# One core, a Mamba-2 and stick-breaking block with SwiGLU: all first products of two gate/up quads run behind the last out_proj block, whose norm and tail go first, and the last tails get buffers of their own

## The chip, the cores and the metric

The kernel runs on one core of a Trainium2 chip. The metric is the device time of one execution in microseconds (us); the kernel before takes 1240.92 us, the median of three runs. In the profile the engines are PE (TensorE, matmuls), PEld (its weight loads), DVE (VectorE), ACT (ScalarE), POOL (GpSimd) and SP (SyncE, which here issues loads). L12 is line 12 of the kernel's file.

## What is computed

The reference is one layer on x of 1024 x 1024 in float32. What lies around the change is its second half:

```python
mix = jnp.concatenate([y_ssd, y_sb], axis=-1) @ w_out[layer]
x = x + rms_norm(mix, post_mix_gain[layer])

h = rms_norm(x, pre_ffn_gain[layer])
f = (jax.nn.silu(h @ w_gate[layer]) * (h @ w_up[layer])) @ w_down[layer]
x = x + rms_norm(f, post_ffn_gain[layer])
```

`y_ssd` is the output of a Mamba-2 scan, `y_sb` that of stick-breaking attention; both are done when the part that matters here begins. w_out is 1024 x 1024, w_gate and w_up are 1024 x 2816, w_down is 2816 x 1024.

## The kernel before, in words

**Numbers and products.** Every operand of a large product is split in two: a cast to a shorter float on ACT gives the high part `hi` (L72), a subtraction on DVE gives the rest `lo` (L73). A product of two such operands is three matmuls, hi·hi, hi·lo and lo·hi, into the same PSUM bank (`mm3`, L76 to L78). So each split costs one ACT and one DVE instruction, and PE cannot start before both.

**Order.** The program is written for a scheduler that places each engine's instructions by their dependencies and by a priority, which is by default the order in which the code is written. Every engine then works through its own list in order and waits by semaphores. Two things alter the order: `tc.high_priority(offset=n)` gives the instructions under it the priority of code written n instructions earlier, and `tc.issue_after(i)` keeps them behind instruction i. SP's list consists of the loads, POOL's of the stores, among other work. A load waits in SP's list until its buffer is free and, where it reads back what was stored, until that store has landed; the loads behind it wait with it.

**out_proj, norms and tails.** The output projection runs in eight blocks of 128 rows, p = 0 to 7, from the last rows of the sequence to the first. `run(p, ...)` is 48 matmuls into two banks `po`, with weights `woh`/`wol` and inputs `yhl`. `out_norm(p)` is a generator in three parts, with a `yield` between them:

1. squares of the product on ACT with row sums (L1035);
2. the inverse root of the row mean (`row_rstd`, the small steps `e`, `y`, `v`, `t`, `r` on ACT and DVE, L859 to L864), then per half the scaling by it and by the gain (DVE, L1041), the addition to x (DVE, L1042) and the squares for the second norm (ACT, L1043), and the store of the new x (POOL, L1044);
3. a second `row_rstd`, and the scaling by the second norm (DVE, L1049), which gives the tile `tm`, kept as `ts[p]`.

`out_tail(sb, ...)` turns block sb = p round: eight PE transposes into two banks `pt` (L1063), copied by ACT into `hT` (L1064). Tails 0 to 3 fill the columns of the operands B11 and B21 and store `hT` to `h2_d` in memory. Tails 4 to 7 load those blocks back as `b11` and `b21` (SP, L1076), form sums and differences with them on DVE (L1078, L1079, L1082, L1083), split two results into T2 and T3, and store three more to `late_d` on POOL (L1077, L1084, L1085). `b11` and `b21` have one buffer each, in the pool `op`, which all four tails share in turn. Tail p - 2 is written behind `run(p)`.

**Gate and up.** h @ w_gate and h @ w_up are made in quads of 256 columns by a scheme of seven products in place of eight (Strassen's). A quad runs once for gate (`g`) and once for up (`u`), and `step(p)` carries both one stage on. One stage is 12 matmuls for each of the two: `pa` = weights times B11, then a second product with B21 into the same bank; `pb` with T2; `pc` with T3; `pe` with T1; then T4 into the bank of `pc`, and B22 into that of `pe`. DVE adds up the parts as they come: `u2` (L911), `u3` (L917 and L921), and the two others (L925, L929). Four results of each quad leave through `gate`: Silu on ACT (L1004), a multiplication on DVE (L1005) and a store on POOL (L1006).

The left operands come from `lops`, a list of split weight blocks. The first four are those of quad 0's first two products, made by `early_ops` from the buffers `er` (loads at L1020, splits into `eo`). All others are made by `left_gen`, which `pump(n)` carries on until n pairs are ready: quad 1's first four from `head` (loads at L940), the rest from `fraw` (loads at L954), with DVE sums `fs` (L966, L967, L970, L972). T1, T4 and B22 are loaded back from `late_d` at the end of this part and split there (L1142 and the line behind it).

**PSUM.** `bank` hands out the eight banks in a fixed ring, two tagged mm, two z, one o and three px; `ring_i` counts them. A bank whose last reader is not through holds up the next product on it.

**The order written out.** Before the change, quad 0's first product `step(0)` stands ahead of block 7, the last; then `run(7)`, tail 5, part 1 of norm 7, the second product of quad 0 (`a00`), `pump(1)`, part 2 of norm 7, tail 6, part 3, `pump(2)`, quad 1's first product `step(1)`, tail 7, the gates. Tail 7 feeds T2, and with it the product `pb` of both quads.

Of the kernel before, what the change touches and what calls it, by code (L numbers as in the profile page):

```python
# [8 lines left out]
F32 = mybir.dt.float32  # L9
# [3 lines left out]
ALU = mybir.AluOpType  # L13
# [3 lines left out]
P = 128  # L17
# [3 lines left out]
NB = S // P  # L21
# [18 lines left out]
SIDE = 1  # L40
WARM = 12
LOOK = 4
# [5 lines left out]
def tile_hybrid_block(  # L48
# [19 lines left out]
    f32 = lambda ap: ap.bitcast(F32)  # L68

# [5 lines left out]
    def mm3(ps, ah, al, bh, bl, start, stop, more=False):  # L75
        T.matmul(ps, lhsT=ah, rhs=bh, start=start, stop=False, skip_group_check=more)  # L76
        T.matmul(ps, lhsT=ah, rhs=bl, start=False, stop=False, skip_group_check=more)  # L77
        T.matmul(ps, lhsT=al, rhs=bh, start=False, stop=stop, skip_group_check=more)  # L78
# [819 lines left out]
    def quad(p, name):  # L898
# [12 lines left out]
        V.tensor_tensor(p1, b, p1, ALU.add)  # L911
# [5 lines left out]
        V.tensor_tensor(u3, c, u2, ALU.add)  # L917
# [61 lines left out]
    def pump(n):  # L979
        while len(lops) < 2 * n:  # L980
            try:
                next(lg)
            except StopIteration:
                break
# [26 lines left out]
    with es_o:  # L1011
# [39 lines left out]

        def out_tail(sb, t):
# [21 lines left out]
            b11, b21 = [op.tile([P, 4, P], F32, tag=x, name=x, bufs=1) for x in ("b11", "b21")]  # L1074
# [23 lines left out]
        for p in range(NB):  # L1098
            if p == NB - 1:
                step(0)  # L1100
            run(p, "late" if p < 2 else "all")
            if p > 1:
                out_tail(p - 2, ts.pop(p - 2))
            norm = out_norm(p)
            if p < NB - 1:
                for _ in norm:
                    pass
            if 2 < p + 2 < NB:
                out_load(p + 2, "all")
            if p == 5:  # L1110
                early_ops()
        es_w.close()
        fw = ctx.enter_context(tc.tile_pool(reuse_waits="tile", name="fw", bufs=1, side="right"))
# [3 lines left out]
        next(norm)  # L1117
        a00 = step(0)
        pump(1)
        next(norm)  # L1120
        out_tail(6, ts[6])
        pump(2)
        next(norm, None)

        ring_i[0] += 4
        step(1)
        out_tail(7, ts[7])
# [9 lines left out]
    for i, op in enumerate((T1, T4, B22)):  # L1137
        if i == 1:
            pump(3)
        for c in range(4):  # L1140
            hi, lo = [x[:, :, P * c : P * c + P] for x in op]
            nc.sync.dma_start(f32(lo), late_d[i][c])  # L1142
            split(hi, lo, f32(lo))

# [229 lines left out]
```

## Time and profile before

| what | value |
|---|---|
| three runs | 1241.06, 1240.9, 1240.92 us (median 1240.92) |
| the profiled execution, its own time | 1240.09 us |
| its span | 1238.4 us |
| mean granted clock of TensorE | 0.989 |

The span is that of the engines' records and leaves out 1.7 us of the execution around them. The stretch that the change moves runs from about 568 to 650 us of the span. Rows of the trace are given as start, busy time (both in us), engine, line, operation, what it writes and what it reads, shape; xN joins N instructions on one row, and a bracket at the end gives the idle time of the engine ahead of it and what ended it. A row that joins several instructions has the sum of their times.

### The profile page before, as it was taken

Reading aid. Unit: us, or ns where it says so; the run is one execution under the profiler, and the core shown is the slowest. Engines: PE = TensorE matmul, PEld = TensorE weight load, DVE = VectorE, ACT = ScalarE, POOL = GpSimd, SP = SyncE. Lnnn points to the kernel's source line nnn. Section 1 sums busy time; section 2 is a strip of 40 time slices with the busy share of each in tenths; the row PEclk is TensorE's granted clock in tenths of the full one; section 3 lists DMA queues with packets and bytes.
Section 4 is the critical chain, followed back from the end, with each engine's and each line's share of the span. In section 5 each row is a group of like instructions: output and inputs, shape, how many; then the busy total and the mean of one; then the engine's idle time right before and its main releaser. Section 6 shows DMA issues by size and latency. Waiting matters only on the chain.

```text
span 1238.4 us, 16320 instructions
## 1 busy us (share of the span) xinstructions
PE 1192.9 (96%) x5641; PEld 972.5 (79%) x5641; DVE 931.1 (75%) x1461; ACT 587.2 (47%) x1115; POOL 92.2 (7%) x232
## 2 busy tenths in 40 slices
PE   9998999999999998999799999999999999999997
PEld 7776778787887775787678888888888888888885
DVE  7478988778997888667898555566655558998777
ACT  7247555555654667445553333333233335444543
POOL 0041110010110100011200000000000000000000
PEclk9999999999999999999999999999999999999998
DMA  6693252445557425855773223222233198133247
GB/s 193 193 353 112 71 153 74 139 118 178 151 167 197 136 83 185 232 179 176 263 220 104 76 79 102 77 85 80 65 102 97 67 325 319 62 126 104 101 136 237
DMA packets 139882, 183.23 MB, mean 148 GB/s; under 512 B 10660, under 2 KB 94852, under 8 KB 139800
## 3 DMA queue, kind: packets, MB, share of 16 engines
q1 hardware_dynamic: 128544, 151.18, 39.8%
q0 software_dynamic: 7424, 25.17, 5.6%
q10 hardware_dynamic: 3832, 5.84, 1.3%
q8 instruction: 44, 0.72, 0.2%
q14 instruction: 38, 0.31, 0.1%
HBM read 132.23 MB, written 49.92 MB: 147 GB/s over the span
## 4 chain that ended last, share of the span: by engine, by line
PE 70%; DVE 11%; issue 8%; DMA 5%; ACT 4%; SPq 1%; POOL 1%; DVEq 0%; ACTq 0%; POOLq 0%
PE pd L76 5%; PE pd L78 5%; PE pd L77 5%; DVE sn L569 3%; PE o L592 2%; PE tp L580 2%; PE pj_x L76 2%; PE pj_x L78 2%; PE pcg L76 2%; PE pj_x L77 2%; PE pcg L77 2%; PE pcg L78 2%; PE pcu L77 2%; PE peu L77 2%; PE peg L77 2%
## 5 line engine op out<-in xcount | busy, mean ns | idle before, releaser
L72 ACT CAST flhi<-fraw 128x512 fp32r<-128x512 f32 x102 | 62.7, 621 | 168.2 <-PE pcg L77 39.6
L76 PE MATMUL pd<-fohi 128*128 128x512 f32 x260 | 101.3, 389 | 0.0
L77 PE MATMUL pd<-folo,fohi 128*128 128x512 f32 x260 | 101.2, 389 | 0.0
L78 PE MATMUL pd<-fohi,folo 128*128 128x512 f32 x260 | 101.2, 389 | 0.0
L569 DVE TENSOR_TENSOR_SCAN sn<-sn,smask 128x1024 f32<-128x1024 f32 (+3 forms) x64 | 87.3, 1365 | 17.6 <-ACT sn L565 17.4
L73 DVE TENSOR_TENSOR fllo<-fraw,flhi 128x512 fp32r<-128x512 f32 x102 | 69.5, 685 | 34.9 <-ACT flhi L72 34.9
L565 ACT ACTIVATE sn<-zp,msc 128x512 f32<-128x512 f32 (+2 forms) x96 | 55.9, 585 | 34.6 <-PE zp L564 28.9
L72 ACT CAST fohi<-rt 128x512 fp32r<-128x512 f32 x83 | 48.8, 618 | 47.9 <-PE pd L77 28.0
L584 ACT CAST wh<-tp 128x512 fp32r<-128x512 f32 (+1 forms) x80 | 42.6, 544 | 38.6 <-PE tp L580 38.1
L73 DVE TENSOR_TENSOR folo<-rt,fohi 128x512 fp32r<-128x512 f32 x83 | 54.8, 682 | 6.5 <-ACT fohi L72 6.5
L72 ACT CAST flhi<-fs 128x512 fp32r<-128x512 f32 x44 | 27.2, 622 | 67.5 <-PE peg L77 33.5
L585 DVE TENSOR_TENSOR wl<-tp,wh 128x512 fp32r<-128x512 f32 (+1 forms) x80 | 49.6, 628 | 10.8 <-ACT wh L584 10.2
L566 ACT ACTIVATE sp<-zp,msc 128x512 f32<-128x512 f32 (+2 forms) x96 | 55.8, 583 | 2.5 <-PE tp L580 2.4
L78 PEld LDWEIGHTS pd<-fohi,folo 128*128 128x128 f32 x260 | 48.8, 188 | 10.2
L77 PEld LDWEIGHTS pd<-folo,fohi 128*128 128x128 f32 x260 | 48.8, 188 | 10.1
L76 PEld LDWEIGHTS pd<-fohi 128*128 128x128 f32 x260 | 48.8, 188 | 10.1
L580 PE MATMUL tp<-ident,sp 128*128 128x128 f32 x288 | 48.0, 278 | 5.7 <-DVE sp L570 5.1
L76 PE MATMUL po<-woh,yhl 128*128 128x512 f32 x128 | 50.9, 398 | 1.8 <-ACT yhl L72 1.3
L1006 POOL DMA_DIRECT2D a_d<-sg x44 | 23.7, 540 | 382.6 <-DVE sg L1005 382.6
L76 PE MATMUL pj_x<-hh,wh_x 128*128 128x512 f32 x128 | 52.2, 408 | 0.0
L78 PE MATMUL po<-woh,yhl 128*128 128x512 f32 x128 | 50.7, 397 | 0.5 <-DVE yhl L73 0.5
L78 PE MATMUL pj_x<-hh,wl_x 128*128 128x512 f32 x128 | 51.1, 399 | 0.0
(425 smaller groups left out, 3469.1 us busy)
## 6 DMA issues: line engine op xcount, KB each, us to landing
ps<-a_d SPq DMA_DIRECT2D x55, 256.0 KB
fraw<-in_w_gate_dram SPq DMA_DIRECT2D x22, 512.0 KB
fraw<-in_w_up_dram SPq DMA_DIRECT2D x22, 512.0 KB
a_d<-sg POOLq DMA_DIRECT2D x44, 256.0 KB, 2.6
rt<-in_w_down_dram SPq DMA_DIRECT2D x33, 256.0 KB
rt<-a_d SPq DMA_DIRECT2D x22, 256.0 KB
ps<-in_w_down_dram SPq DMA_DIRECT2D x22, 256.0 KB
xt<-in_x_t_dram SPq DMA_DIRECT2D x8, 512.0 KB
```

The costliest lines, as they stand in the source:

```text
L72: A.copy(hi, src)
L73: V.tensor_tensor(lo, src, f32(hi), ALU.subtract)
L76: T.matmul(ps, lhsT=ah, rhs=bh, start=start, stop=False, skip_group_check=more)
L77: T.matmul(ps, lhsT=ah, rhs=bl, start=False, stop=False, skip_group_check=more)
L78: T.matmul(ps, lhsT=al, rhs=bh, start=False, stop=stop, skip_group_check=more)
L565: A.activation(sn[:, 1 + off : 1 + off + cw_], zp[:, 0:cw_], AF.Sigmoid, scale=rqn[:, qb : qb + 1])
L566: A.activation(sp[:, off : off + cw_], zp[:, 0:cw_], AF.Sigmoid, scale=rqp[:, qb : qb + 1])
L569: V.tensor_tensor_scan(sn[:, 1 : 1 + W], sn[:, 1 : 1 + W], smask[:, 0:W], 1.0, ALU.mult, ALU.max)
L580: T.transpose(tp[:, P * i : P * i + P], ws[a][:, co : co + P], ident)
L584: A.copy(wh[:, 0:n_], tp[:, 0:n_])
L585: V.tensor_tensor(wl[:, 0:n_], tp[:, 0:n_], f32(wh[:, 0:n_]), ALU.subtract)
L592: T.matmul(o[:, 0:cw_], lhsT=vv[:, k, h, :], rhs=wt[:, c0 : c0 + cw_], start=(first and k == kb + 1 and wt is wh), stop=(last and k == kb ...
```

## The change

- Block 7's matmuls move ahead of quad 0's first product, and tail 5 with them: now `run(7)`, part 1 of norm 7, tail 5, `step(0)`, part 2, tail 6, part 3, then `step(0)`, `pump(2)`, `step(1)`, tail 7 and the gates.
- The three parts of norm 7 have a raised priority (150), and so has tail 7, which is kept behind the last matmul written so far.
- Tails 5, 6 and 7 take `b11` and `b21` from a new pool `op2` with two buffers each.
- The twelve loads of T1, T4 and B22 are issued together. The splits of T4 and of B22 are put further back: each behind `pump(1 + LOOK)`, a step of quad 0 with its gate, and the last DVE addition of that step.
- The ring of banks skips two places instead of four.

```diff
+URGENT = 150
...
-        T.matmul(ps, lhsT=al, rhs=bh, start=False, stop=stop, skip_group_check=more)
+        last_mm[0] = T.matmul(ps, lhsT=al, rhs=bh, start=False, stop=stop, skip_group_check=more)
...
         product(b, lops[x], T2, True)
-        V.tensor_tensor(p1, b, p1, ALU.add)
+        evac[0] = V.tensor_tensor(p1, b, p1, ALU.add)
...
-        V.tensor_tensor(u3, c, u2, ALU.add)
+        evac[0] = V.tensor_tensor(u3, c, u2, ALU.add)
...
-            b11, b21 = [op.tile([P, 4, P], F32, tag=x, name=x, bufs=1) for x in ("b11", "b21")]
+            late = op2[0] if op2 else op
+            b11, b21 = [late.tile([P, 4, P], F32, tag=x, name=x, bufs=2 if op2 else 1) for x in ("b11", "b21")]
...
-        for p in range(NB):
-            if p == NB - 1:
-                step(0)
+        for p in range(NB - 1):
             run(p, "late" if p < 2 else "all")
             if p > 1:
                 out_tail(p - 2, ts.pop(p - 2))
-            norm = out_norm(p)
-            if p < NB - 1:
-                for _ in norm:
-                    pass
+            for _ in out_norm(p):
+                pass
             if 2 < p + 2 < NB:
                 out_load(p + 2, "all")
             if p == 5:
                 early_ops()
+
+        run(NB - 1, "all")
         es_w.close()
+        op2.append(es_o.enter_context(tc.tile_pool(reuse_waits="tile", name="op2", bufs=2, side="left")))
...
-        next(norm)
+        norm = out_norm(NB - 1)
+        with tc.high_priority(offset=URGENT):
+            next(norm)
+        out_tail(5, ts.pop(5))
+        step(0)
+        with tc.high_priority(offset=URGENT):
+            next(norm)
+        out_tail(6, ts[6])
+        with tc.high_priority(offset=URGENT):
+            next(norm, None)
         a00 = step(0)
-        pump(1)
-        next(norm)
-        out_tail(6, ts[6])
         pump(2)
-        next(norm, None)
-
-        ring_i[0] += 4
         step(1)
-        out_tail(7, ts[7])
+        with tc.high_priority(offset=URGENT), tc.issue_after(last_mm[0].ins):
+            out_tail(7, ts[7])
+
+        ring_i[0] += 2
...
     for i, op in enumerate((T1, T4, B22)):
-        if i == 1:
-            pump(3)
+        for c in range(4):
+            nc.sync.dma_start(f32(op[1][:, :, P * c : P * c + P]), late_d[i][c])
+
+    def late_split(op):
         for c in range(4):
             hi, lo = [x[:, :, P * c : P * c + P] for x in op]
-            nc.sync.dma_start(f32(lo), late_d[i][c])
             split(hi, lo, f32(lo))
...
+    late_split(T1)
+    for op in (T4, B22):
+        pump(1 + LOOK)
+        gate(step(0))
+        with tc.issue_after(evac[0].ins):
+            late_split(op)
```

The changed file has two to seven more lines ahead of these places, so that L1041 becomes L1043 there, L1049 becomes L1051, L1063 becomes L1067, L1076 becomes L1081, L1079 becomes L1084, L1083 becomes L1088, L76 becomes L78 and L1142 becomes L1149.

PE, behind block 6's matmuls. `pt_5874` and `pt_5880` are tail 4's two banks, `pag` the bank of quad 0's first gate product, `po_59..` block 7's. Before, quad 0 comes first:

```order
L1063 MATMUL pt_5874<-ident_66,tm_5635 128x128 x4
L1063 MATMUL pt_5880<-ident_66,tm_5635 128x128 x4
L76 MATMUL pag_5937<-B11h_5118,eo_5801 128x512
L77 MATMUL pag_5937<-B11l_5119,eo_5801 128x512
L78 MATMUL pag_5937<-B11h_5118,eo_5802 128x512
```

After the change block 7 follows tail 4:

```order
L1067 MATMUL pt_5874<-ident_66,tm_5635 128x128 x4
L1067 MATMUL pt_5880<-ident_66,tm_5635 128x128 x4
L78 MATMUL po_5937<-woh0_4966,yhl_5786 128x512
L79 MATMUL po_5937<-wol0_4967,yhl_5786 128x512
L80 MATMUL po_5937<-woh0_4966,yhl_5786 128x512
```

The 24 matmuls of quad 0's first product have moved from ahead of block 7's 48 to behind them and behind tail 5's transposes.

DVE, in norm 7, from its additions to x (L1042, after L1044) to the scaling by the second norm (L1049, after L1051). `pt_6118`, `hT_6116` and `b21_6131` are tail 6's, `fs` are sums of quad 0's weights, `sg_6224` the multiplication of a gate. Before:

```order
L1042 TENSOR_TENSOR x1_6052<-x1_6052,tm_6055 128x512 x2
L1079 TENSOR_TENSOR pt_6118<-pt_6124,b11_6130 128x512
L1082 TENSOR_TENSOR hT_6116<-hT_6116,b11_6130 128x512
L861 SCALAR_TENSOR_TENSOR v_6153<-ssq2_6108,e_6156 128x1
L966 TENSOR_TENSOR fs_6274<-fraw_6266,fraw_6268 128x512
L73 TENSOR_TENSOR T2l_5123<-pt_6118,T2h_5122 128x4x128
L73 TENSOR_TENSOR T3l_5125<-pt_6124,T3h_5124 128x4x128
L1083 TENSOR_TENSOR b21_6131<-b21_6131,pt_6118 128x512
L862 SCALAR_TENSOR_TENSOR t_6155<-y0_6154,v_6153 128x1
L967 TENSOR_TENSOR fs_6275<-fs_6274,fraw_6266 128x512
L864 SCALAR_TENSOR_TENSOR r_6161<-t_6155,y0_6154 128x1
L1005 TENSOR_TENSOR sg_6224<-pau_5952,sg_6224 128x512
```

After the change; `pt_6004`, `pt_6010` and `b21_6017` are tail 5's, `pt_6087` is tail 6's, `head_6144` quad 1's first weight block:

```order
L1044 TENSOR_TENSOR x1_5997<-x1_5997,tm_6000 128x512 x2
L75 TENSOR_TENSOR T2l_5123<-pt_6004,T2h_5122 128x4x128
L75 TENSOR_TENSOR T3l_5125<-pt_6010,T3h_5124 128x4x128
L863 SCALAR_TENSOR_TENSOR v_6108<-ssq2_6071,e_6111 128x1
L1088 TENSOR_TENSOR b21_6017<-b21_6017,pt_6004 128x512
L864 SCALAR_TENSOR_TENSOR t_6110<-y0_6109,v_6108 128x1
L1083 TENSOR_TENSOR pt_6087<-pt_6087,hT_6079 128x512
L866 SCALAR_TENSOR_TENSOR r_6116<-t_6110,y0_6109 128x1
L75 TENSOR_TENSOR fllo_6153<-head_6144,flhi_6152 128x512
L1051 SCALAR_TENSOR_TENSOR tm_6000<-x1_5997,r_6116,g2_b_5132 128x512 x2
```

Eight large instructions stood inside norm 7 between these two points, five do now; most of tail 6 and the gate's multiplication have moved behind it, tail 5's end has moved in.

SP, from the last load of `er` on. Before:

```order
L1076 DMA b11_6030<-h2_d0_1_140 128x512
L1076 DMA b21_6031<-h2_d1_1_144 128x512
L940 DMA head_6082<-in_w_gate_dram 128x4x128
L940 DMA head_6083<-in_w_up_dram 128x4x128
L940 DMA head_6084<-in_w_gate_dram 128x4x128
L940 DMA head_6085<-in_w_up_dram 128x4x128
L954 DMA fraw_6266<-in_w_gate_dram 128x4x256
L1076 DMA b11_6130<-h2_d0_2_141 128x512
L954 DMA fraw_6268<-in_w_gate_dram 128x4x256
L954 DMA fraw_6270<-in_w_up_dram 128x4x256
L954 DMA fraw_6272<-in_w_up_dram 128x4x256
L1076 DMA b21_6131<-h2_d1_2_145 128x512
```

After:

```order
L1081 DMA b11_6016<-h2_d0_1_140 128x512
L1081 DMA b21_6017<-h2_d1_1_144 128x512
L1081 DMA b11_6093<-h2_d0_2_141 128x512
L1081 DMA b21_6094<-h2_d1_2_145 128x512
L942 DMA head_6144<-in_w_gate_dram 128x4x128
L942 DMA head_6145<-in_w_up_dram 128x4x128
L942 DMA head_6146<-in_w_gate_dram 128x4x128
L1081 DMA b11_6212<-h2_d0_3_142 128x512
L942 DMA head_6147<-in_w_up_dram 128x4x128
L956 DMA fraw_6270<-in_w_gate_dram 128x4x256
L956 DMA fraw_6272<-in_w_gate_dram 128x4x256
L956 DMA fraw_6274<-in_w_up_dram 128x4x256
```

Tail 6's loads now stand right behind tail 5's, ahead of the weights of both quads, and tail 7's `b11` among quad 1's; before, each of them waited for the buffer of the tail ahead of it.

More of the change, by code (lines that the diff above doesn't have):

```diff
@@ L68, in tile_hybrid_block @@
     f32 = lambda ap: ap.bitcast(F32)
+    last_mm, evac = [None], [None]
     def split(hi, lo, src):
@@ L1050, in out_norm @@
             ts[p] = t
+        op2 = []
         def out_tail(sb, t):
```

## The prediction, made before the changed kernel was run

> **What bounds the kernel now.** I read the page's busy shares first, then the waits of PE over the stretch that the change touches, then PE's rows in order of time, then the granted clock, and last the DVE and ACT rows that PE waited for.
>
> ```profile
> span 1238.4 us, 16320 instructions
> PE 1192.9 (96%) x5641; PEld 972.5 (79%) x5641; DVE 931.1 (75%) x1461; ACT 587.2 (47%) x1115; POOL 92.2 (7%) x232
> ```
>
> PE is the bound over the whole, so only PE's idle and slowed time can be won. The waits of PE between 560 and 700 us are five:
>
> ```profile
> PE pt L1063 <- DVE tm L1049: 2.9, 1, 2.9
> PE pbg L76 <- ACT T2h L72: 2.8, 1, 2.8
> PE pag L76 <- DVE tm L1041: 2.6, 1, 2.6
> PE pcg L76 <- DVE u3g L917: 2.1, 1, 2.1
> PE pbu L76 <- ACT flhi L72: 0.7, 1, 0.7
> ```
>
> Their places, in PE's rows by time:
>
> ```profile
> 568.64 1.03 PE L1063 MATMUL pt<-ident,tm 128*128 128x128 f32 x8
> 572.24 0.47 PE L76 MATMUL pag<-B11h,eo 128*128 128x512 f32 x1 [2.56 <-DVE tm L1041]
> 573.63 0.63 PE L78 MATMUL pag<-B11h,eo 128*128 128x512 f32 x1
> 574.06 0.63 PE L76 MATMUL pag<-B11h,eo 128*128 128x512 f32 x1
> 579.37 0.39 PE L76 MATMUL po<-woh,yhl 128*128 128x512 f32 x1
> 590.26 1.03 PE L1063 MATMUL pt<-ident,tm 128*128 128x128 f32 x8
> 591.05 0.48 PE L76 MATMUL pag<-B21h,eo 128*128 128x512 f32 x1
> 610.98 1.09 PE L1063 MATMUL pt<-ident,tm 128*128 128x128 f32 x4 [2.91 <-DVE tm L1049]
> 616.57 0.50 PE L76 MATMUL pbg<-T2h,flhi 128*128 128x512 f32 x1 [2.79 <-ACT T2h L72]
> 637.90 0.59 PE L76 MATMUL pcg<-T4h,flhi 128*128 128x512 f32 x1 [2.09 <-DVE u3g L917]
> 650.49 0.39 PE L76 MATMUL pbg<-T2h,flhi 128*128 128x512 f32 x1
> ```
>
> Block 7 of out_proj is 48 matmuls from 579.37 to 590.26, so 0.227 us each; eight transposes take 0.79 (590.26 to 591.05). From 568.64 to 650.49, where quad 1's second product starts, PE issues 48 + 4x24 + 5x24 = 264 matmuls and 32 transposes: 59.9 + 3.2 = 63.1 us at that pace. It takes 81.85, so 18.8 us are lost. Of these, 2.8 (569.43 to 572.24) and 1.7 (the 24 matmuls to 579.37 take 7.13, not 5.45: they start 0.43 apart at 573.63) lie ahead of everything that moves. That leaves at most 14.3 us to win.
>
> The slowed matmuls come from the clock, read in slices of 3.41 us (columns: us, then busy us of PE, PEld, DVE, ACT, POOL, then PEclk, DMA share, GB/s):
>
> ```profile
> 91.96:95.37 3.41, 1.85 (x8) 0.90 (x6) 1.46 (x2) 1.90 (x4) 0.65 (x2) 1.00 1.01 345
> 95.37:98.79 3.42, 1.45 (x7) 1.15 (x7) 0.89 (x1) 3.41 (x6) 0.28 (x1) 1.00 0.73 246
> 98.79:102.20 3.41, 3.41 (x11) 2.46 (x11) 3.21 (x3) 2.23 (x5) 0.72 (x2) 0.50 0.00 0
> 481.08:484.49 3.41, 1.65 (x9) 1.05 (x8) 3.41 (x6) 3.41 (x4) 0.00 (x0) 1.00 0.42 119
> 484.49:487.90 3.41, 3.41 (x8) 2.74 (x9) 3.41 (x3) 2.67 (x4) 0.00 (x0) 0.50 0.90 339
> 638.09:641.50 3.41, 3.41 (x9) 2.63 (x9) 3.41 (x7) 1.25 (x2) 0.00 (x0) 0.50 0.17 54
> ```
>
> A slice with PE busy 1.85 us left the next at full clock; one with 1.65 halved it for 3.41 us. So idle of some 1.6 to 1.8 us in one slice costs a further 1.7 us.
>
> What PE waited for is norm 7, the last block's, and then a full DVE:
>
> ```profile
> 569.64 0.62 ACT L72 CAST eo<-er 128x512 fp32r<-128x512 f32 x1 [3.41 <-DMA er<-in_w_gate_dram]
> 582.22 0.62 ACT L72 CAST eo<-er 128x512 fp32r<-128x512 f32 x1 [0.16 <-DMA er<-in_w_up_dram]
> 582.80 0.75 DVE L1041 SCALAR_TENSOR_TENSOR tm<-po,r,gm_b 128x512 f32<-128x512 f32 x1
> 589.50 1.41 DVE L1049 SCALAR_TENSOR_TENSOR tm<-x,r,g_b 128x512 f32<-128x512 f32 x2
> 591.85 0.62 ACT L1035 ACTIVATE tm<-po 128x512 f32<-128x512 f32 x1
> 599.46 1.40 DVE L1041 SCALAR_TENSOR_TENSOR tm<-po,r,gm_b 128x512 f32<-128x512 f32 x2
> 600.77 1.28 DVE L1042 TENSOR_TENSOR x<-x,tm 128x512 f32<-128x512 f32 x2
> 602.84 8.89 SPq L1076 DMA_DIRECT2D b<-h_d  x3
> 608.09 0.69 DVE L1083 TENSOR_TENSOR b<-b,pt 128x512 f32<-128x512 f32 x1 [2.96 <-DMA b<-h_d]
> 610.09 1.41 DVE L1049 SCALAR_TENSOR_TENSOR tm<-x,r,g_b 128x512 f32<-128x512 f32 x2
> 623.62 1.89 DVE L73 TENSOR_TENSOR fllo<-fraw,flhi 128x512 fp32r<-128x512 f32 x3
> 637.07 0.68 DVE L917 TENSOR_TENSOR u3g<-pcg,p1g 128x512 f32<-128x512 f32 x1
> ```
>
> Block 7 leaves PE at 590.26, ACT squares it from 591.85, DVE scales it at 599.46 (L1041), and the last scaling by the second norm (L1049) ends at 611.50: 21.2 us for a chain of small steps, because DVE and ACT take other rows in between, and because DVE stands 2.96 us before tail 6's b21 (L1083), whose load waits for the single buffer. DVE's step is 0.60 us (three in 1.89, the last 0.69).
>
> **The change, part by part**, placed against this execution (1240.09 us, 1.7 above its span; the median 1240.92 is 0.83 higher). I walked the changed rows of PE, ACT, DVE and SP in their order, gave each the duration and step of its like above, and let each start at the later of its engine's turn and its operands.
>
> 1. Block 7 before quad 0's first product. It inherits the wait at 572.24 (same PSUM bank, same scaling of block 5) and the slowed clock, and ends at 572.24 + 7.13 + 24x0.227 = 584.8 instead of 590.26: 5.45 us earlier. The first product pays for it: its banks are now those of block 6, whose scaling on DVE falls from 582.80 to about 585.1, behind the two splits of tail 4, the fourth eo split and b21 (four steps, 2.4 us). PE is free at 585.6 and starts at 586.0: 0.4 idle.
>
> 2. Norm 6 ends where it did (about 590.8, row 589.50 + 1.41): the scaling starts later, but its two halves no longer have those four steps between them.
>
> 3. Norm 7, first half. ACT cannot square block 7 before norm 6 is through with ACT (588.9), so it does it at 589.4 instead of 591.85; the first scaling follows on DVE behind three ops of tail 5, at 593.6 instead of 599.46: 5.9 us earlier.
>
> 4. Norm 7, second half. Before, 8.0 us from the end of L1042 (602.05) to L1049 (610.09): eight DVE steps of 0.60, three small ones, and the 2.96 of b21. Now five steps and the three small ones stand there (two splits, b21, a subtraction, a head split), none on a late load: 596.2 to 599.7, 3.5 us. The own buffers do this: the h2 loads of tails 5 and 6 stand right behind the er loads on SP and wait only for an er buffer (free at about 580.2), so they land some 585.5 at the latest, with the 5.2 us from 602.84 to 608.09 as the worst landing that a row shows; they are needed at 592.2. Gain of the second half: 4.5 us. So L1049 ends at 601.1, 10.4 earlier.
>
> 5. From there to u3g, whose read frees the bank for T4, DVE is full. Before: 611.50 to 637.75, 26.25. Now 45 steps of 0.60 = 27.1: tail 6's end and three head splits have moved behind the norm, four B22 splits have moved behind u3g. A loss of 0.85. The covers: fraw (SP 594.5, needed at 606.4), the T1 and T4 loads (the last one waits for tail 7's store at about 613.2 + 2.6, needed at 620 and 624), and ACT, which runs one to four steps ahead. The twelve loads now stand ahead of quad 1's fraw on SP; those issue from 618.5, and are needed at 630.4. On POOL block 7's x1 store now stands ahead of tail 5's b21 store, which tail 7's b21 load and, behind it on SP, the first T1 load wait for: that load lands near 604 and is needed at 612.4. So nothing is charged for the queues.
>
> 6. PE in that time: 0.4 at 586.0, then 1.5 at 598.3 (the third matmul of quad 1's first product needs the head split that sits in norm 7), 0.4 at 602.5 and 0.3 at 611.7, and none for T4, since pe ends at 628.1, as u3g does. T4 thus starts at 628.2 instead of 637.90. Without 2.1 us idle before it, no half clock follows: 48 matmuls take 10.9, not 12.6 (637.90 to 650.49), another 1.7.
>
> Sum: 5.9 + 4.5 - 0.85 + 1.7 = 11.3 us (part 1 is inside the 5.9). PE's side agrees: 63.1 + 4.5 + 2.6 of idle from 568.64 puts quad 1 at 638.8, against 639.1. Behind it the two programs issue the same work, and no wait of PE follows until 700, so I let the gain reach the end.
>
> A walk has no room for handovers that slip; the 12 between ACT and DVE in parts 3 and 4 at 0.05 each are 0.6 (an estimate). I take 10.7 off the median: 1230.2. Ends: 11.3 plus the 1.5 us idle not happening, 1228; 10.7 less one halved slice and 2 us of late loads, 1234.
>
> On the clock a page speaks. The Trainium skill, TensorE: Matmul & The Clock Gate, section "Why this matters for your kernels", advises against idle gaps over about 3 us. By that none of the gaps here, 2.91 at most, would halve the clock, and the last 1.7 of the sum would be no gain: 1231.9. The trace disagrees: 2.09 us at 637.90 was followed by 0.50.
>
> **Rivals.**
> - The clock halves once more. The 1.5 us idle at 598.3 lies just under the 1.6 to 1.8; a slip of 0.3 in the norm's chain tips it. Price 1.7 + 0.3: 1232.2. For it: the head split sits at the end of norm 7. The slices run on a fixed beat (98.79, 484.49 and 638.09 are whole multiples of 3.413 apart), so the gap lies wholly in the one from 597.1 to 600.5. Against it: that leaves PE busy 1.9 us there, and 1.85 did not halve it.
> - DVE gives the gain back. It is busy through here:
>
> ```profile
> 620.00:630.00 10.00, 10.00 (x43) 8.13 (x43) 8.54 (x15) 6.74 (x12) 0.00 (x0) 0.95 1.06 278
> 630.00:640.00 10.00, 7.91 (x32) 5.97 (x31) 9.38 (x16) 4.79 (x9) 0.00 (x0) 0.91 0.99 275
> 640.00:650.00 10.00, 10.00 (x42) 8.24 (x41) 10.00 (x18) 5.30 (x10) 0.54 (x1) 0.92 0.39 123
> ```
>
>   Its work is the same, so PE can win no more than DVE's idle time shrinks. If T1's, T4's and fraw's loads crowd (DMA share is near 1 already), DVE waits again for them: half the gain, 1235.5.
> - Slower than before: norm 7 queues behind a load. On DVE the changed order puts tail 5's b11 (its add) ahead of norm 7's scaling, and PE has step(1) behind that. Every us that this load lands after 592.2 is lost. It decides at 592.2 + 11.3 = 603.5, 23 us after its issue, against a worst 5.2 seen; two us past that point the time is 1243.
> - Nothing changes, because what ends last is the stretch from L1049 to T4, whose 27.1 us the change does not shorten: but its start moves with L1049, so parts 3 and 4 would have to fail: 1240.9.
>
> **How the numbers follow.** Base walk (1228 to 1231.7) 0.62; one more halved slice (to 1232.5) 0.18; DVE gives back (1233 to 1238) 0.13; unchanged 0.03; slower 0.04. The predicted time is the base's, 1230.2. The range 1227.3 to 1234.5 leaves out the far half of the third case and the last two, and a little below the walk. 0.2% is 2.5 us, about what a measurement of this kernel can tell from no change; faster 0.93, same 0.03, slower 0.04.
>
> **What would show it.** Step 1: the last out_proj matmul at about 585, the first product right behind tail 5's transposes. Steps 3 and 4: norm 7's scaling near 593.6, its L1049 rows ending near 601, no DVE wait on an h2 load. Step 5: DVE without idle from 598 to 634, u3g near 628. Step 6: PE's waits for tm, T2h and u3g gone; one of 1 to 2 us for a head split at 598; the clock at 0.50 only once between 560 and 700. Wrong, if DVE waits for a T1l or T4l load, if the wait for the head split passes 1.8, or if quad 1 starts 11 us earlier and the end does not.

## The result and the profile after

The changed kernel took 1233.68 us (median of six executions, 1230.38 to 1236.6) and the kernel before 1241.57 (six, 1240.9 to 1242.94, among them the three known ahead of the forecast). The ratio is 0.9935, with a 95% interval of 0.9919 to 0.9951: 8.1 us won, with 6.1 to 10.1 as the interval. The forecast was 10.7 us won and 1230.2. The sign, the range and, but for one step, the mechanism hold. The central value is 3.5 us too low: 0.65 of that is the kernel before, whose median was 1240.92 in the forecast, and the rest a gain that is smaller than forecast; 10.7 lies just outside its interval. One execution of a later run, the kernel before with T4's wait filled, took 4092.08 us and is left out of that run's ratio.

The head of the page of the kernel after, whose profiled execution took 1233.45 us:

```profile
span 1231.7 us, 16326 instructions
PE 1189.5 (97%) x5641; PEld 968.1 (79%) x5641; DVE 929.9 (75%) x1461; ACT 586.2 (48%) x1115; POOL 92.1 (7%) x232
```

The work is the same (5641 matmuls, 1461 DVE instructions); PE is busy 3.4 us less, as it would be with fewer matmuls at half clock (the mean granted clock is 0.995 instead of 0.989), and idle 3.3 us less. The waits of PE from 560 to 700 us, in the columns of the five shown of before:

```profile
PE po L78 <- DVE tm L1043: 3.0, 1, 3.0
PE pag L78 <- DVE tm L1043: 1.9, 1, 1.9
PE pbg L79 <- DVE T2l L75: 0.7, 1, 0.7
PE pbg L78 <- ACT T2h L74: 0.6, 1, 0.6
PE pag L80 <- DVE fllo L75: 0.6, 1, 0.6
```

The 2.9 us for tail 7's transposes and the 2.1 us for u3g are gone, and the 2.8 us for T2 is 0.6 + 0.7. What is left stands at the start: 3.0 us ahead of block 7 (which now inherits the wait that quad 0's first product had) and 1.9 ahead of that product, both for a norm's scaling on DVE, which reads the bank that PE writes next. PE's rows by time:

```profile
570.71 1.03 PE L1067 MATMUL pt<-ident,tm 128*128 128x128 f32 x8
574.77 0.47 PE L78 MATMUL po<-woh,yhl 128*128 128x512 f32 x1 [3.03 <-DVE tm L1043]
585.78 1.03 PE L1067 MATMUL pt<-ident,tm 128*128 128x128 f32 x8
588.67 0.47 PE L78 MATMUL pag<-B11h,eo 128*128 128x512 f32 x1 [1.86 <-DVE tm L1043]
614.46 0.50 PE L78 MATMUL pbg<-T2h,flhi 128*128 128x512 f32 x1 [0.63 <-ACT T2h L74]
631.96 0.47 PE L78 MATMUL pcg<-T4h,flhi 128*128 128x512 f32 x1
642.93 0.39 PE L78 MATMUL pbg<-T2h,flhi 128*128 128x512 f32 x1
```

The stretch from tail 4's transposes to quad 1's `pb` product (what the prediction calls its second product), 81.85 us before, is now 72.22 (570.71 to 642.93), against the floor of 63.1. Outside it no difference goes with the order: the way to its start takes 568.6 to 573.6 us over all profiles of this document, the two orders mixed, and the way from its end to the end of the span takes 587.9 to 588.8 in all but the one without the raised priority, where PE's order is another at that place. The profiled execution of before reached the stretch early (568.64), so in what follows a time of after is put on the clock of before by taking off 2.07 us.

DVE's rows that answer to those of before, by time; a row of x2 starts with the first half:

```profile
587.78 1.41 DVE L1043 SCALAR_TENSOR_TENSOR tm<-po,r,gm_b 128x512 f32<-128x512 f32 x2
592.06 1.42 DVE L1051 SCALAR_TENSOR_TENSOR tm<-x,r,g_b 128x512 f32<-128x512 f32 x2
595.83 1.40 DVE L1043 SCALAR_TENSOR_TENSOR tm<-po,r,gm_b 128x512 f32<-128x512 f32 x2
601.61 1.41 DVE L1051 SCALAR_TENSOR_TENSOR tm<-x,r,g_b 128x512 f32<-128x512 f32 x2
611.29 0.69 DVE L968 TENSOR_TENSOR fs<-fraw 128x512 f32<-128x512 f32 x1 [1.55 <-DMA fraw<-in_w_up_dram]
631.13 0.68 DVE L919 TENSOR_TENSOR u3g<-pcg,p1g 128x512 f32<-128x512 f32 x1
```

The first two rows are norm 6, the next two norm 7. Norm 7's last scaling starts at 599.54 on the clock of before instead of 610.09. The fifth row is a wait that the prediction did not have.

### The profile page after: what moved, and what is told of

The parts are those of the page before. It is cut to its first block, busy times and chain, and to the rows that moved or that the text cites. A ratio compares the mean times of both kernels' runs of the same rounds, so it can differ in the third digit from the quotient of the medians.

```text
span 1231.7 us, 16326 instructions
## 1 busy us (share of the span) xinstructions
PE 1189.5 (97%) x5641; PEld 968.1 (79%) x5641; DVE 929.9 (75%) x1461; ACT 586.2 (48%) x1115; POOL 92.1 (7%) x232
## 4 chain that ended last, share of the span: by engine, by line
PE 70%; DVE 13%; DMA 7%; ACT 4%; issue 4%; SPq 1%; POOL 0%; DVEq 0%; ACTq 0%; POOLq 0%
PE pd L79 5%; PE pd L78 5%; PE pd L80 5%; DVE sn L571 3%; DMA Rb<-r_d 3%; PE o L594 2%; PE tp L582 2%; PE pj_x L78 2%; PE pcg L78 2%; PE pj_x L80 2%; PE pcg L80 2%; PE peg L80 2%; PE pcu L80 2%; PE peu L80 2%; PE peu L78 2%
## 5 line engine op out<-in xcount | busy, mean ns | idle before, releaser
L78 PE MATMUL pd<-fohi 128*128 128x512 f32 x260 | 101.1, 389 | 0.0
L571 DVE TENSOR_TENSOR_SCAN sn<-sn,smask 128x1024 f32<-128x1024 f32 (+3 forms) x64 | 87.3, 1366 | 17.8 <-ACT sn L567 17.7
L78 PE MATMUL po<-woh,yhl 128*128 128x512 f32 x128 | 51.0, 399 | 7.1 <-DVE tm L1043 3.7
L79 PEld LDWEIGHTS pd<-folo,fohi 128*128 128x128 f32 x260 | 48.8, 188 | 10.7 <-DVE folo L75 0.7
L78 PEld LDWEIGHTS pd<-fohi 128*128 128x128 f32 x260 | 48.8, 188 | 10.2
L80 PEld LDWEIGHTS pd<-fohi,folo 128*128 128x128 f32 x260 | 48.8, 188 | 10.1
L78 PE MATMUL pj_x<-hh,wh_x 128*128 128x512 f32 x128 | 52.4, 409 | 0.0
```

The lines of the kernel that those rows point to most:

```text
L80: last_mm[0] = T.matmul(ps, lhsT=al, rhs=bh, start=False, stop=stop, skip_group_check=more)
L571: V.tensor_tensor_scan(sn[:, 1 : 1 + W], sn[:, 1 : 1 + W], smask[:, 0:W], 1.0, ALU.mult, ALU.max)
```

## The experiments

The yardstick in all of them is the same stretch: 81.85 us before, 72.22 after. Two profiles of one kernel differ by 0.2 and 1.2 us in it, as the first experiment shows, so about 1 us between single profiles says nothing. The theory is that of the prediction: the gain is norm 7's shorter chain on DVE, and the half clock that goes with the wait at T4. Ratios are to the kernel before, timed in the same session.

**Both kernels once more.** A stretch seen once in each kernel is a thin base, so both were profiled again, without an edit.

> The kernel before once more, unchanged, for a second profile of it. What the first showed from tail 4's transposes to quad 1's pb product: 81.85 us, with four slow slices of 3.41 us, begun at whole multiples of that. Theory (the beat's place differs from run to run, so that the same idle time falls into one slice in one run and into two in the next): the slow slices begin elsewhere, there are one to three of them, and the stretch takes 78 to 81 us. Rival (the first profile was typical): 81.85 within 0.5 us and slow slices at the same places.

```profile
571.54 1.03 PE L1063 MATMUL pt<-ident,tm 128*128 128x128 f32 x8
653.61 0.39 PE L76 MATMUL pbg<-T2h,flhi 128*128 128x512 f32 x1
```

82.07 us (1244.14 us for the execution). Four slices at half clock stand in this part of it again, from about 576.0, 613.6, 620.4 and 641.0 us. Counted from tail 4's transposes these are the places of the first profile (573.2, 610.8, 617.6 and 638.0 there): the rival holds, and the first profile was typical.

> The changed kernel once more, unchanged, for a second profile of it. The first had no slow slice in the same stretch and took 72.22 us, though PE stood idle for 3.3 us ahead of block 7. Theory (those 3.3 us lay across two slices): with the beat at another place they halve the clock behind them in this run or do not, 72.2 or 73.9 us; the time is 1230 to 1236 by that and by the wait for the row scales at 504. Rival (the clock does not fall behind this wait at all): 72.2 within 0.3 us.

PE's rows of the second profile of after:

```profile
570.91 1.03 PE L1067 MATMUL pt<-ident,tm 128*128 128x128 f32 x8
574.06 0.72 PE L78 MATMUL po<-woh,yhl 128*128 128x512 f32 x1 [2.11 <-DVE tm L1043]
587.93 0.47 PE L78 MATMUL pag<-B11h,eo 128*128 128x512 f32 x1 [0.24 <-DVE tm L1043]
641.91 0.39 PE L78 MATMUL pbg<-T2h,flhi 128*128 128x512 f32 x1
```

71.00 us (1231.86 us), less than either forecast. The two profiles of after differ most in one place, which the slices show (the columns of the prediction): the first two lines are of the first profile, the other two of the second.

```profile
569.79:573.20 3.41, 1.96 (x13) 1.50 (x11) 0.37 (x1) 0.81 (x2) 0.00 (x0) 1.00 0.61 217
573.20:576.61 3.41, 1.83 (x8) 1.56 (x9) 3.22 (x7) 0.69 (x3) 0.00 (x0) 1.00 0.28 77
```

```profile
570.72:574.13 3.41, 1.30 (x11) 0.99 (x9) 1.95 (x5) 0.81 (x2) 0.00 (x0) 1.00 0.15 55
574.13:577.54 3.41, 3.41 (x8) 2.69 (x9) 2.17 (x5) 2.33 (x8) 0.54 (x1) 0.50 0.37 119
```

A wait of 3.03 us that lay across two slices left 1.96 and 1.83 us of PE's work in them and halved nothing; one of 2.11 in a single slice left 1.30 and halved the next. Yet the run with the halved slice lost nothing by it: block 7 ended later against its start, and the first product, which waits for norm 6 anyway, then waited 0.24 instead of 1.86 (588.67 - 570.71 = 17.96 us in the one, 587.93 - 570.91 = 17.02 in the other).

So the means are 81.96 and 71.6: 10.3 us won in the stretch, by two profiles each.

**The own buffers alone left out.** On after:

```diff
-        op2.append(es_o.enter_context(tc.tile_pool(reuse_waits="tile", name="op2", bufs=2, side="left")))
```

> The changed kernel with one thing undone: tails 5 to 7 share the single b11 and b21 again. The order of PE, ACT and DVE stays that of the changed kernel; on SP the loads of tail 6 and 7 move behind quad 1's and part of quad 0's weights. Theory of the prediction (the own buffers carry the second half of norm 7, because without them DVE stands about 3 us before a b21): 3 to 4.5 us of the gain go, 1237 to 1238. Rival (the new order alone does it: tail 5's last read of b11 is at 595.9 and of b21 at 600.3, and tail 6 needs the reloaded ones only at 602.9 and 607.1, so a load of 5 us is in time): the changed kernel's 1233.7 within 1 us.

1237.62 us, ratio 0.9965 [0.995, 0.9979]; the stretch is 76.96, 4.7 us more than after's. SP, ACT, PE and DVE, in this order:

```profile
584.64 6.27 SPq L1081 DMA_DIRECT2D b<-h_d  x2
591.03 0.44 SPq L942 DMA_DIRECT2D head<-in_w_gate_dram  x1
596.00 0.62 ACT L74 CAST flhi<-head 128x512 fp32r<-128x512 f32 x1 [2.28 <-DMA head<-in_w_gate_dram]
598.70 0.80 PE L78 MATMUL pag<-B21h,eo 128*128 128x512 f32 x1 [3.67 <-ACT p1g L907]
603.44 0.16 DVE L863 SCALAR_TENSOR_TENSOR v<-ssq,e 128x1 f32<-128x1 f32 x1 [2.99 <-ACT e L861]
612.95 0.69 DVE L1088 TENSOR_TENSOR b<-b,pt 128x512 f32<-128x512 f32 x1 [1.80 <-DMA b<-h_d]
```

The first row is tail 5's loads: b21 cannot issue until the one buffer is free, and holds SP for 6.27 us. Behind it stand the weights of quad 1, which issue at 591.03 instead of 584.66, so ACT waits 2.28 us for a `head`, its copy of p1g behind that is late, and PE waits 3.67 us for the bank. The late ACT holds up norm 7 too: DVE waits 2.99 us for it inside the norm, whose second scaling starts at 605.52 instead of 601.61. The buffers are worth 4.7 us by the stretch and 3.9 by the times, so the size forecast (3 to 4.5) is right, but the way is another: what costs is not a b21 that DVE waits for inside norm 7, but a load that has no buffer and holds up loads of something else on the queue. DVE does wait 1.80 us for tail 6's b21 (the last row), but behind the norm.

**The same buffers alone, on before.** `op2` is opened behind the last out_proj block, and tails 6 and 7 take `b11` and `b21` from it:

```diff
-            b11, b21 = [op.tile([P, 4, P], F32, tag=x, name=x, bufs=1) for x in ("b11", "b21")]
+            late = op2[0] if op2 else op
+            b11, b21 = [late.tile([P, 4, P], F32, tag=x, name=x, bufs=2 if op2 else 1) for x in ("b11", "b21")]
...
+        op2.append(es_o.enter_context(tc.tile_pool(reuse_waits="tile", name="op2", bufs=2, side="left")))
```

> The kernel before with one part of the change alone: tails 6 and 7 get buffers of their own (two each), nothing else. Theory (DVE's wait of 2.96 us for tail 6's b21 is on the path): it goes, the second scaling of norm 7 and all behind it come 2.5 to 3 us earlier, 1238.7. Rival (DVE then waits as long for the next load, since the weights of quad 0 now stand behind the h2 loads on SP, or the scaling's wait is filled by other steps): 1241.6 within 0.8 us.

1239.91 us, ratio 0.9983 [0.9969, 0.9998]: 2.1 us won (0.2 to 3.8). In before's order the buffers take away the 2.96 us that DVE stood in norm 7 for b21, but from 595 to 615 us it now waits 1.6 us for a `fraw` and 1.3 for ACT, and PE's waits for tail 7's rows and for T2 stay at 2.4 and 2.9. Less than the removed wait reaches the end. The profile's stretch, 77.74, is 4.1 to 4.3 less than before's two; that is one execution, and the timed interval does not reach so far.

**The raised priority left out.** On after:

```diff
-URGENT = 150
+URGENT = 0
```

> The changed kernel with the raised priority set to 0, so that norm 7 and tail 7 stand where they are written. On DVE norm 7's first scaling then comes four steps later, and ten large steps instead of five stand between its additions and its second scaling. Theory (the chain through norm 7 sets when T2 is ready and so the end): nine steps of 0.60 us later at the second scaling, 5.4 us; the same nine steps are gone behind it, of which tail 7 can use those that stood ahead of its first subtraction, seven: the price is 1.2 to 2.5 us, 1235 to 1236. Rival (DVE is full up to the first u3 in either order and does the same work there, so only its idle time counts): 1233.7 within 0.8 us.

1237.53 us, ratio 0.9961 [0.9947, 0.9976]: 3.8 us of after's gain, more than the 1.2 to 2.5 expected. Norm 7 on DVE in this run:

```profile
597.16 1.41 DVE L1043 SCALAR_TENSOR_TENSOR tm<-po,r,gm_b 128x512 f32<-128x512 f32 x2
605.95 1.40 DVE L1051 SCALAR_TENSOR_TENSOR tm<-x,r,g_b 128x512 f32<-128x512 f32 x2
```

Against after (595.83 and 601.61) the first half is 1.3 us later and the second 4.3: without the priority other rows slip back between the additions and the second scaling. PE then waits 1.8 us for tail 7's transposes and 2.8 for T2. So norm 7's second half counts for the end, as part 4 has it, but not us for us: counted from tail 4's transposes T2's product starts 1.8 us later than in after (616.25 less 570.68 is 45.57, against 43.75). The other 2 us come behind it: the wait for T2 is followed by half clock from about 616.2 to 619.6 us, and PE waits 1.2 us for T1's splits. The edit also takes the priority from tail 7 and changes PE's order behind T4, so it is not a test of norm 7 alone.

**The late loads and splits in before's order.** On after, the loop of T1, T4 and B22 as it was (each load ahead of its split, no step of quad 0 kept ahead of the splits):

```diff
+    for i, op in enumerate((T1, T4, B22)):
+        if i == 1:
+            pump(3)
+        for c in range(4):
+            hi, lo = [x[:, :, P * c : P * c + P] for x in op]
+            nc.sync.dma_start(f32(lo), late_d[i][c])
+            split(hi, lo, f32(lo))
...
```

> The changed kernel with T1, T4 and B22 loaded and split in the order of the kernel before: the four B22 splits stand ahead of the first u3 on DVE again, not behind it. Theory (DVE is full to u3, which T4's first matmul waits for): u3 is 4 steps of 0.60 us later, T4 waits 2.3 us where the changed kernel has no wait, 1236.1; if that idle time halves the clock for one slice of 3.41 us as before the change, 1237.8. Rival (the gain at this place comes from norm 7 alone and DVE has slack by then): 1233.7 within 0.8 us.

1236.21 us, ratio 0.9948 [0.9928, 0.9968]; the stretch is 76.54, 4.3 more than after's. PE's row and the slices behind it:

```profile
633.72 0.47 PE L78 MATMUL pcg<-T4h,flhi 128*128 128x512 f32 x1 [2.34 <-DVE u3g L919]
```

```profile
631.09:634.50 3.41, 1.07 (x6) 0.68 (x5) 3.41 (x7) 0.00 (x0) 0.00 (x0) 1.00 0.85 271
634.50:637.91 3.41, 3.41 (x10) 2.64 (x9) 3.41 (x7) 1.25 (x2) 0.00 (x0) 0.50 0.01 5
```

The wait for u3g is back and halves the next slice. DVE shows no wait from 614.24 to u3g at 632.89, with the four B22 splits just ahead of it (628.68 to 631.77). So moving them behind u3g is what keeps DVE in time for T4, as part 5 has it: 2.34 us of wait and 1.6 of half clock (12.58 us from T4 to quad 1 instead of 10.97), about 4 of the 4.3. The timed difference to after is 2.5 us; the two intervals overlap, so its size is not settled by the times.

**The half clock alone, on before.** Eight matmuls of no use, ahead of the T4 product, fill PE's wait there:

```diff
+            if p == 0 and x == 0:
+                for _ in range(8):
+                    T.matmul(b, lhsT=B21[0][:, 0, 0:P], rhs=B21[0][:, 0, :], start=True, stop=True)
```

> The kernel before with work added: eight matmuls of 128x512 on operands that are there, into quad 0's bank of its pb product (read by then), right ahead of T4's first matmul, where PE stands idle for 2.09 us and runs at half clock behind it. Nothing else changes. Clock theory (the slice from 634.9 to 638.3 has PE busy for 1.3 us only, and that is what halves the next): eight at 0.23 us fill it to more than 1.85, the clock stays at full, and from tail 4's transposes to quad 1's pb product it takes 80.1 us in place of 81.85; the time falls by 1.7 to 1239.9. Rival (the clock falls for another reason, or what was added holds T4 up): 81.85 or more, 1241.6 or more.

```profile
634.38 1.98 PE L925 MATMUL pbg<-B21h 128*128 128x512 f32 x8
636.65 0.47 PE L76 MATMUL pcg<-T4h,flhi 128*128 128x512 f32 x1 [0.30 <-DVE u3g L917]
```

The wait is filled to 0.30, and from quad 0's `pb` product to quad 1's it takes 32.27 us (615.38 to 647.65) against 33.92 and 33.80 in before's two profiles: 1.6 won in the profile, as the clock's price of 1.7 says. The times do not show it: 1241.03 us, ratio 1.0 [0.9989, 1.0012], and 1.7 us would be 0.9986, just outside. The profile, taken of the fastest of the twelve executions (1237.48 us), speaks for the term and the times against it, so what the half clock alone is worth stays open.

**The two waits that are left.** Both stand behind ACT:

```profile
572.18 0.62 ACT L74 CAST eo<-er 128x512 fp32r<-128x512 f32 x1 [3.36 <-DMA er<-in_w_gate_dram]
581.44 0.62 ACT L74 CAST eo<-er 128x512 fp32r<-128x512 f32 x1 [2.91 <-DMA er<-in_w_gate_dram]
582.45 0.60 ACT L1037 ACTIVATE tm<-po 128x512 f32<-128x512 f32 x1
```

ACT stands 3.36 and 2.91 us before casts of weights that have not landed, with norm 6's squares queued behind the second. The `er` loads shared a buffer and could only follow each other. Here each gets its own place in T3h's memory, which is free until then:

```diff
-        raw = wo_tile([P, 4, 256], "er")
+        er = rpA.tile([P, 4, 4, P], F32, tag="T3h", name="er")
...
+        raw = er[:, 2 * dh + si]
```

> The changed kernel with quad 0's first weights (the er loads) put where T3's high part will be written by tail 4, four places in place of one that they shared in turn, so that ACT finds them there: in the changed kernel ACT waits 3.36 us at 572.18 and 2.91 at 581.44 for such a load, with norm 5's and norm 6's steps behind it, and PE waits 3.03 for the one and 1.86 for the other. Theory (these two waits of PE are the rest of what can be won here): PE starts block 7 about 3 us earlier and the first product follows without a wait, 4.5 to 5 us in all, 72.2 becomes 67.5, and the time 1229. Rival A (DVE is full from 597 on, so that what PE wins ahead comes back as waits for T2 and u3): at most 2 us, 1231.7 or more. Rival B (the four loads now stand on SP ahead of block 6's inputs): blocks 5 or 6 wait for theirs, and the time is not below 1233.

1225.66 us, ratio 0.987 [0.9857, 0.9883]: 8.0 us below after, where 4.5 to 5 were expected. The stretch is 64.14, one us over the floor. The only wait of PE from 560 to 700, then PE's and ACT's rows:

```profile
PE pbg L79 <- DVE T2l L75: 0.2, 1, 0.2
```

```profile
572.14 1.03 PE L1068 MATMUL pt<-ident,tm 128*128 128x128 f32 x8
572.93 0.48 PE L78 MATMUL po<-woh,yhl 128*128 128x512 f32 x1
573.85 0.61 ACT L1038 ACTIVATE tm<-po 128x512 f32<-128x512 f32 x1
584.71 0.48 PE L78 MATMUL pag<-B11h,eo 128*128 128x512 f32 x1
```

Norm 6's squares run at 573.85 instead of 582.45, and both waits for a scaling go, with most of the 1.9 us that PE waited for a head split and T2. The same edit on before:

> The kernel before with the er loads put where T3's high part will be written, as in the version that gained about 8 us on the changed kernel, and nothing else. Theory (the load that ACT stood before was a loss of its own, whatever the order behind it): PE's wait of 2.56 us at 572.24 goes, and with it the halved slice behind it where it falls in one; norm 7 starts that much earlier: 2.6 to 4 us, 1237.5 to 1239. Rival (in the old order norm 7 and a full DVE end last, and what PE wins at 572 it waits at tail 7's transposes): 1241.5 within 1 us, so that only the new order can use it.

1236.25 us, ratio 0.9968 [0.9954, 0.9983]: 4.0 us, half as much. PE gets past its first product without the wait of 2.56 us, and the three waits behind it stay:

```profile
607.12 0.63 PE L1064 MATMUL pt<-ident,tm 128*128 128x128 f32 x4 [2.57 <-DVE tm L1050]
611.92 0.50 PE L76 MATMUL pbg<-T2h,flhi 128*128 128x512 f32 x1 [3.26 <-ACT T2h L72]
633.09 0.47 PE L76 MATMUL pcg<-T4h,flhi 128*128 128x512 f32 x1 [1.98 <-DVE u3g L917]
```

They are 7.8 us in sum, as in before (2.91, 2.79 and 2.09), and they are the three that the change takes away. By the times the order of the change and the earlier weights are worth 8.1 and 4.0 us alone and 15.8 together (1241.45 less 1225.66); by the stretch 10.3 and 5.8 (81.96 less 76.12) alone and 17.8 together. So they add up, and gain a little more together, if the difference is more than the scatter.

**A third buffer.** After's DVE stood 1.55 us before the last `fraw`, whose load stands on SP behind tail 7's loads. On after:

```diff
-            ... bufs=2 if op2 else 1) ...
+            ... bufs=3 if op2 else 1) ...
```

> The changed kernel with three buffers each for b11 and b21 in the new pool in place of two, so that tail 7 waits for none. In the changed kernel tail 7's b11 load waits on SP from 586.3 to 595.93 for tail 5's buffer, and quad 1's last head load and quad 0's four fraw loads stand behind it (596.3 to 600.0); DVE waits 1.55 us for the last fraw at 611.29. Theory: the fraw loads issue some 9 us earlier, that wait goes, and the time falls by 1 to 1.5 us, 1232.4. Rival (the loads were bound by the DMA engines and not by their issue, and now crowd the head loads that quad 1's first product needs at 600): no gain or up to 1 us loss, 1233.7 to 1234.7.

1233.33 us, ratio 0.9933 [0.992, 0.9945], after's own; the stretch is 73.29. The wait for `fraw` is gone, and SP has a new one:

```profile
SPq L1149 <- DMA late_d<-b: 20.9, 1, 20.9
```

```profile
616.57 2.79 SPq L1149 DMA_DIRECT2D T1l<-late_d  x4
```

T1's loads begin at 616.57 instead of 609.04, behind the store of a `b` tile (POOL issues tail 7's last at 614.14). So the place that T1 takes seems to be held by the third buffer until tail 7's b21 is stored; the trace shows the wait, not the place. DVE waits 1.3 us for T1 instead. With the `er` edit as well:

> The changed kernel with both: the er loads in T3's place, and three buffers each for b11 and b21. Theory (two independent waits): the gains add, 6 us below the changed kernel, 1227.7. Rival (DVE is the bound behind norm 7 and one gain uses up the other): as the better of the two alone.

1227.75 us, ratio 0.9888 [0.9875, 0.99], stretch 65.53: the third buffer is worth nothing here either, and beside the 1225.66 of the `er` edit alone it rather costs 2 us (each of the four executions is slower than each of the four there).

**A slow slice ahead of the stretch.** PE waits 2.58 us at 504.61 in after, and a slice that begins between 504.8 and 507.8 runs at half clock in 10 of the 13 profiles taken up to here (not in before's first, with a wait of 1.35 us there, nor in that with the third buffer alone, 1.16, nor in that of the `er` edit on before, where 2.38 us of wait lay across two slices). On after with the `er` edit, eight matmuls of no use are put ahead of that block of out_proj:

```diff
+            if p == 0:
+                fill = psum("o", "fill")
+                with tc.issue_after(last_mm[0].ins):
+                    for _ in range(8):
+                        T.matmul(fill, lhsT=woh[0][:, 0:P], rhs=woh[0][:, 0:512], start=True, stop=True)
```

> The version with the er loads in T3's place (1225.7), with work added at another stall, which the change does not touch: eight matmuls of 128x512 on out_proj's weights into a spare bank, right ahead of block 0's last twelve, where PE stands 1.2 to 4.4 us before a load of row scales near 504 in every profile, and where the slice of 3.41 us behind it ran at half clock in all profiles but two. Clock theory (idle time within one slice is what halves the next): the eight at 0.23 us leave 0.6 to 1.3 us idle, no slow slice near 505 remains, and the time falls by up to 1.7, to 1224.2. Rival (the clock falls for another reason, or the added work holds the late matmuls up in most runs): a slow slice remains or the time is 1225.7 or more.

The slices of the `er` edit without the fill, and below them those with it:

```profile
504.00:507.41 3.41, 1.00 (x5) 0.37 (x3) 2.85 (x12) 2.05 (x5) 0.00 (x0) 1.00 0.53 96
507.41:510.82 3.41, 3.41 (x9) 2.68 (x9) 2.02 (x4) 2.70 (x5) 0.00 (x0) 0.50 1.05 370
```

```profile
503.18:506.59 3.41, 3.41 (x17) 2.66 (x15) 2.69 (x11) 2.00 (x5) 0.00 (x0) 1.00 0.62 165
506.59:510.00 3.41, 3.41 (x15) 2.71 (x15) 2.26 (x5) 3.05 (x7) 0.00 (x0) 1.00 0.98 335
```

The half clock is gone there. The time, 1224.79 us (1222.48 to 1225.98; ratio 0.9856 [0.9831, 0.988]), lies 0.9 below that without the fill, which the intervals do not tell apart. These two are the fastest versions found: the `er` edit beats before and after by its interval, and what the fill adds is not settled.

## Why the prediction came out as it did

Times of after are on before's clock, the first profile's first and the second's (2.27 taken off) behind it.

1. Block 7 and the first product: block 7's end forecast at 584.8, found at 583.7 and 584.4; the first product at 586.0, found at 586.6 and 585.7. The wait there, 0.4 in the forecast, was 1.86 and 0.24: it takes up whatever block 7's clock gives. Block 7's half clock, which the forecast carried over, came in the second profile and not in the first.
2. Norm 6's end: 590.8 forecast, 591.4 found in the first profile.
3. Norm 7's first scaling: 593.6 forecast, 593.8 and 592.8 found. This is the largest term of the sum, 5.9 us, and it holds (5.7 and 6.6).
4. L1051's end: 601.1 forecast, 601.0 and 600.0 found. The end holds and the stated cause only in part. Leaving the priority out makes this end 4.3 us later and the kernel 3.8 slower, and leaving the buffers out 3.9 later and 3.9 slower, so the chain counts, if not us for us. But "The own buffers do this" is too simple: without them the loss comes over SP, `head`, ACT and a PSUM bank.
5. The way to u3g's end: 628.1 forecast, 629.7 and 628.5 found. The step that failed is its cover for `fraw` ("SP 594.5, needed at 606.4"). The first load issued as forecast, at 594.8; but the last two issued only from 596.9 (598.96 in after's own time), behind quad 1's weights and tail 7's b11, and DVE got the last at 611.29, 11 to 12 us later, with the DMA share at 0.92 to 1.06 from 597 to 612 us. The only landing that the prediction has is the 5.2 us of an h2 load. DVE stood 1.55 and 1.22 us for it. So the rival "DVE gives the gain back" came true in the small: 1.2 to 1.6 us, not 5.
6. PE's waits: the 1.5 forecast for the head split was 0.56 and 0.58, the 0.7 behind it 1.3 and 1.04 at T2, and none at T4. The waits miss in both directions; that their sum with the first product's, 3.7 and 1.9 us, lies around the 2.6 forecast is partly luck. The full clock behind T4 is there: 48 matmuls take 10.97 us (631.96 to 642.93), 10.9 forecast. By the rule of the Trainium skill that the prediction weighed (TensorE: Matmul & The Clock Gate, "Why this matters for your kernels", no gaps over about 3 us) this was no gain. The wait of 2.34 us in the run with the late loads in before's order, followed by half clock, disagrees with that rule once more.

The rival of a half clock at 598 did not come. The argument that placed it carried the beat of before's profile over to the changed kernel, and that was wrong: the slice that is slow near 505 us starts at 505.0, 505.8 and 507.4 in three executions of changed kernels, which are not whole multiples of 3.413 apart, so the beat has another phase in each. The Trainium skill says as much (TensorE: Matmul & The Clock Gate, "Part 1: The HAM clock gate": a free-running window), and the trace agrees.

For the sum: the stretch gained 9.6 us by the first profiles and 10.3 by the means of two, against 11.3 for the walk and 10.7 for the forecast. The mis-sized term is the loss of 0.85 in part 5: from the end of norm 7 to u3g's end it took 28.8 and 28.5 us instead of 27.1, a loss of 2.5 and 2.2, and the `fraw` wait of 1.55 and 1.22 is nearly all of the difference. The timed gain is 8.1 [6.1, 10.1], and the spans of the two profiles each (1238.4 and 1242.4, 1231.7 and 1230.1) give 9.5, inside that. Of the 0.8 us between stretch and spans, 0.7 is the way to the stretch, longer by that in after's two profiles (570.8 us on the mean) than in before's (570.1), where single profiles of one kernel differ by up to 2.9. Whether the rest up to the timed 8.1 is a loss elsewhere or the scatter of six executions is not settled.

## What to carry to other kernels

When a chain of small steps sets the end, look at what else stands in each engine's row between its links; putting that row in order was worth 3.8 us here by one constant, part of it through the clock. A load without a free buffer costs more than its own wait, because the queue holds everything behind it (6.27 us on SP here, and 3.9 us of the time): look on the queue, not at the reader, for what a second buffer is worth, and at what the added buffer's place was to hold next. After a chain is shortened, look at its start: earlier loads into a place of their own were worth 4.0 us in the old order and 8.0 in the new.

## What the hardware showed that was not expected

- The clock goes by the work in one slice of 3.41 us, not by the length of a gap. In the 13 profiles without the last fill, from 480 to 665 us, each slice at full clock with less than about 1.4 us of PE's work was followed by one at half clock, and none with about 1.8 us or more was; between these it went either way, the slices' places being known to about 0.2 us only. A wait of 3.03 us split over two slices (1.96 and 1.83 us busy) cost nothing, while 2.11 (1.30 busy) and 2.34 us (1.07 busy) each halved the next slice. Since the beat has another phase in each execution, the same wait can cost 1.7 us in one and nothing in the next.
- A halved slice costs nothing where PE waits for another engine behind it anyway (the second profile of after, 17.02 us against 17.96).
- Filling a wait with matmuls of no use kept the clock at 1.00 (the slice from 506.59 us in the last run), which removes the slow slice; a gain in the timed median was not shown by either fill.
